# Thirteen no-operations at the head of GpSimd's program: row sums of reciprocals on one core

## The chip, the cores and the metric

The kernel runs on one core of one Trainium2 chip. A core has five engines with an instruction stream each: TensorE (PE), VectorE (DVE), ScalarE (ACT), GpSimd (POOL) and SyncE (SP). They meet at semaphores. SyncE issues the transfers between main memory and the on-chip memory of 128 partitions; sixteen DMA engines carry them. The metric is the device time of one execution in microseconds (us), as the median of several runs.

## The reference

```python
"x": np.abs(np.random.randn(32, 512, 1024)).astype(np.float32) + 1e-6

def reference(x):
    return np.sum(1.0 / x, axis=-1).astype(np.float32)
```

16,384 rows of 1,024 numbers, 64 MiB in all, are read; each row gives the sum of its reciprocals, and 64 KiB are written. The scheme leaves 128 rows of 1,024 numbers to each partition. The text calls them rows 0 to 127, and a "row" is then a tile of 128 partitions by 1,024 numbers.

## The kernel before, in words

A ring of 46 row slots (`ring`) holds the input; `sums` takes one column per row. No engine divides. ScalarE computes the reciprocal square root of a row in place (operation `A`, line 178), and somebody squares and adds it:

- `Z` (line 188): ScalarE squares and adds up itself.
- `G` and `T`: GpSimd squares the row in place (line 281), VectorE adds up (line 284).
- `Q` (line 241): VectorE squares and adds up in one instruction.
- `B` (line 256), with `K` and `M`: VectorE takes mean and variance of half rows, from which the sum of squares follows at the end.
- `P`, `U`, `L`, `E`, `R`, the pair path: 1/a + 1/b = (a + b)/(ab). GpSimd multiplies the left half of a row by its right half (`P`, line 195) into one of five product buffers (`prod`). TensorE adds the two halves by two multiplications with the identity matrix into a bank of its result memory (`U`, line 202). ScalarE turns the product into its reciprocal in two steps (`L` and `E`, line 212), and VectorE multiplies by the sum of halves and adds up (`R`, line 221). ScalarE has 512 elements twice instead of 1,024 once and a squaring.

Row 127 is split in two halves of 512 numbers.

The order is written out by hand in `PLAN`, a list of tokens; the letter is the operation, the number the row, `+n` a count of rows and `@n` the buffer or the bank. Each engine executes its own tokens in the list's order. `D` (line 170) is a load of so many rows on SyncE's queue. A load waits until the ring slots that it overwrites are free. The helper `note` drops waits that follow from others.

Where an instruction needs more semaphores than it can wait for by itself, the compiler puts wait words ahead of it, instructions of their own in the engine's program (EVENT_SEMAPHORE in the trace, "POOLq" where they are GpSimd's). A word is one instruction of a program. Counted from the head of GpSimd's program, the product of row 111 (token `P111@0`) is word 70 in the kernel before, with a wait word right ahead of it; the product of row 95 (`P95@0`) stands 13 words earlier: six products and squares and six wait words lie between the two.

The part of the list around both products:

```python
R89 B90 A92+2 P95@0 U95@5 R91 A94 B92
G93 L95 B94 A96 A97 T93 A98 B96 E95
...
L109 B106 E107 E109 R107 P111@0 U111@2 A110 B108 A112 P113@1 R109
U113@3 L111 B110 L113 E111 B112 E113
```

GpSimd's program begins with four constants and the identity matrix (`make_identity`: a memset at masks.py:197 and a select at masks.py:199, which needs a setting of the engine ahead of it). Its first square, `G1+3`, waits for ScalarE.

Of the kernel before, what the change touches and what calls it, by code (L numbers as in the profile page):

```python
# [11 lines left out]
def kernel(  # L12
# [5 lines left out]
    nc = tc.nc  # L18
    f32 = mybir.dt.float32
    P = 128  # L20
    NOPS = 0
    D = 1024
    H = D // 2
    F = 128
# [4 lines left out]
    NR = 127  # L29
    STATS = ((43, 3, 11), (80, 2, 18),)  # L30
    STORES = (0, 21, 43, 64, 81, 99, 116)
    LATE = ("A", 127)
    S = float(2**17)
    FIT = 1.0 - 2.0**-17

# [57 lines left out]
    def parse(tok):  # L93
        body, _, b = tok[1:].partition("@")
        r, _, n = body.partition("+")  # L95
        return tok[0], int(r), int(n or 1), int(b or 0)
# [4 lines left out]
    def area(u, n=1):  # L101
        r, at, w = place(u)
        if u >= NR:
            w, n = sum(place(i)[2] for i in range(u, u + n)), 1
        return ring[:, r % R : r % R + n, at : at + w]
# [5 lines left out]
    def note(engine, inst, reads=(), writes=()):  # L111
        inst = inst.ins
        known = dict(begun.get(engine, {}))  # L113
        before = {}
        for spaces, writing in ((reads, False), (writes, True)):
            for space in spaces:
                for other in history.get(space, ()):
                    if writing or other[3]:
                        before[other[0].name] = other
        needed = sorted(before.values(), key=lambda o: -o[4])  # L120
        for other in needed:
            o_inst, o_engine, o_tick, _, _, o_known = other
            if o_engine == engine:
                continue
            if o_tick <= known.get(o_engine, 0):
                tc.declare_no_dep(inst, o_inst, reason="implied by other waits")
                continue
            for e, t in o_known.items():
                known[e] = max(known.get(e, 0), t)
            known[o_engine] = max(known.get(o_engine, 0), o_tick)  # L130
        count[engine] = count.get(engine, 0) + 1
        begun[engine] = known
        entry = (engine, count[engine])
        if engine == "SP":
            entry = (f"load {count[engine]}", 1)
        for spaces, writing in ((reads, False), (writes, True)):
            for space in spaces:
                history.setdefault(space, []).append(
                    (inst, *entry, writing, sum(count.values()), known)
                )  # L140

    def rows(u, n=1):
        spaces = []
        for r, at, w in (place(i) for i in range(u, u + n)):
            spaces += [("row", r % R, i) for i in range(at, at + w, 128)]
        return spaces
# [1 line left out]
    def half(u, at):  # L148
        return [("row", u % R, i) for i in range(at, at + H, 128)]

    work = {}
    loaded = 0
    summed = set()
    slot, bank = {}, {}
# [1 line left out]
    def store(lo, hi):  # L156
        a, at = divmod(lo, HALF)
        nc.sync.dma_start(out=out_v[a, :, at : at + hi - lo], in_=sums[:, lo:hi])

    with tc.manual_schedule():  # L160
        for op, u, n, b in (parse(tok) for tok in PLAN):
            if op == "D":
                n, u = u, loaded
                while n:
# [3 lines left out]
                    if u >= NR:  # L168
                        w, k = sum(place(i)[2] for i in range(u, u + m)), 1
                    inst = nc.sync.dma_start(  # L170
                        out=area(u, m),
                        in_=x_v[r // HALF, :, r % HALF : r % HALF + k, at : at + w],
                    )
                    note("SP", inst, writes=rows(u, m))
                    u, n = u + m, n - m
                loaded = u
            elif op in "AC":
                inst = nc.scalar.activation(  # L178
                    out=area(u, n),
                    in_=area(u, n),  # L180
                    func=Arsqrt if op == "A" else Square,
                    scale=FIT if op == "A" else 1.0,
                )
                note("ACT", inst, writes=rows(u, n))
                work[op, u] = inst.ins
            elif op == "Z":
                r = place(u)[0]
                inst = nc.scalar.activation(  # L188
                    out=area(u), in_=area(u), func=Square, accum_out=sums[:, r : r + 1]
                )  # L190
                summed.add(r)
                note("ACT", inst, writes=rows(u))
            elif op == "P":
                slot[u], r = b, u % R
                inst = nc.gpsimd.tensor_tensor(  # L195
                    out=prod[:, b], in0=ring[:, r, :H], in1=ring[:, r, H:], op=mult
                )
                note("POOL", inst, rows(u), [("slot", b)])
            elif op == "U":
                bank[u], r = b, u % R  # L200
                for h in range(2):
                    inst = nc.tensor.matmul(  # L202
                        ps[:, b],
                        lhsT=ident,
                        rhs=ring[:, r, h * H : (h + 1) * H],
                        start=h == 0,
                        stop=h == 1,
                    )
                    note("PE", inst, half(u, h * H), [("bank", b)])
            elif op in "LE":  # L210
                pair = prod[:, slot[u]]
                inst = nc.scalar.activation(  # L212
                    out=pair,
                    in_=pair,
                    func=Arsqrt if op == "L" else Square,
                    scale=S * FIT if op == "L" else 1.0,
                )
                note("ACT", inst, writes=[("slot", slot[u])])
            elif op == "R":
                pair = prod[:, slot[u]]  # L220
                inst = nc.vector.tensor_tensor_reduce(  # L221
                    out=pair,
                    in0=pair,
                    in1=ps[:, bank[u]],
                    scale=S,
                    scalar=0.0,
                    op0=mult,
                    op1=add,
                    accum_out=sums[:, u : u + 1],
                )  # L230
                note("DVE", inst, [("bank", bank[u])], [("slot", slot[u])])
            elif op == "Q":
                r, at, w = place(u)
                joined = [u]
                while len(joined) < n:
# [5 lines left out]
                inst = nc.vector.tensor_tensor_reduce(  # L241
                    out=row,
                    in0=row,
                    in1=row,
                    scale=1.0,
                    scalar=total if r in summed else 0.0,
                    op0=mult,
                    op1=add,
                    accum_out=total,
# [3 lines left out]
            elif op == "B":  # L253
                i = stat_rows.index(u)
                for h in range(2):
                    inst = nc.vector.bn_stats(  # L256
                        out=stats[:, i, h], in_=ring[:, u % R, h * H : (h + 1) * H]
                    )
                    note("DVE", inst, reads=half(u, h * H), writes=[("stat", i)])
            elif op in "KM":  # L260
                lo, step, n = STATS[u]
                i = stat_rows.index(lo)
                part = stats[:, i : i + n]
                if op == "K":
                    mean = part[:, :, :, :, 1].rearrange("p f h e -> p (f h e)")
                    inst = nc.scalar.activation(  # L266
                        out=mean, in_=mean, func=Square, scale=float(H // 2) ** 0.5
                    )
                    engine = "ACT"
                else:  # L270
                    inst = nc.vector.tensor_reduce(  # L271
                        out=sums[:, lo : lo + step * (n - 1) + 1 : step],
                        in_=part[:, :, :, :, 1:].rearrange("p f h e k -> p f (h e) k"),
                        axis=mybir.AxisListType.XY,
                        op=add,
                    )
                    engine = "DVE"
                note(engine, inst, writes=[("stat", j) for j in range(i, i + n)])
            elif op == "G":
                row = area(u, n)  # L280
                inst = nc.gpsimd.tensor_tensor(out=row, in0=row, in1=row, op=mult)  # L281
                note("POOL", inst, writes=rows(u, n))
            elif op == "T":
                inst = nc.vector.tensor_reduce(  # L284
                    out=sums[:, u : u + n],
                    in_=area(u, n),
                    axis=mybir.AxisListType.X,
                    op=add,
                )
# [2 lines left out]
                for lo, hi in zip(STORES, STORES[1:]):  # L292
                    store(lo, hi)
        store(STORES[-1], F)
        for i in range(NOPS):
            inst = nc.gpsimd.nop(hint="idle", nofuse=True)
            if i == 0:
                tc.add_manual_dep(
                    inst.ins,
                    work[LATE].name,  # L300
                    mybir.DependencyInfo(
                        mybir.DependencyClass.Sync, mybir.DependencyReason.DATA
                    ),
                    reason="GpSimd idles behind the loads",
                )


# [28 lines left out]
```

## Time and profile before

| | |
|---|---|
| median of 3 runs | 166.45 us (166.45 to 166.57) |
| time of the profiled execution | 166.35 us |
| its span, first to last instruction | 164.5 us |
| ACT busy | 145.8 us, 89% |
| DVE busy | 116.0 us, 71% |
| POOL busy | 109.2 us, 66% |
| DMA, all sixteen engines | 408 GB/s over the span |

The profile is one execution. Times in it are microseconds from the start of the span. In a timeline a row is "start, duration, engine, line, operation, output<-input, count, and in brackets the engine's idle time before it and what ended it". Rows of one kind that follow each other without a gap are merged (`x2`). A `q` behind an engine's name is its sequencer, which reads the program and holds the waits. The chain of work that ended last is followed back from the last instruction; "issue" in it is time in which an engine waited for nothing that the profile shows.

A share of the DMA queues in a window is the time of the packets that start in it, over sixteen times the window. It is over 100% for a window shorter than its packets. "q1" carries loads and stores, "q14" instructions.

### The profile page before, as it was taken

How to read it: one execution, taken by the hardware profiler on the slowest of the kernel's cores; microseconds unless marked ns; L12 is line 12 of the kernel's file. 1: busy time of each engine (PE TensorE's matmuls, PEld its weight loads, DVE VectorE, ACT ScalarE, POOL GpSimd, SP SyncE). 2: the span in 40 equal slices, each digit the busy share in tenths (PEclk: the TensorE clock that was granted, in tenths of full speed). 3: DMA queues.
4: the chain of work that ended last, by engine and by line, in shares of the span. 5: the costliest groups of instructions: out<-in, count | busy, mean ns of one | idle time of the engine just before them, and what ended most of it. 6: DMA issues, size and time to landing. Idle time of an engine off the chain costs nothing.

```text
span 164.5 us, 627 instructions
## 1 busy us (share of the span) xinstructions
PE 38.9 (24%) x68; PEld 14.6 (9%) x68; DVE 116.0 (71%) x147; ACT 145.8 (89%) x148; POOL 109.2 (66%) x56
## 2 busy tenths in 40 slices
PE   0000000000000000062000000075808199699600
PEld 0000000000000000020000000031302133234100
DVE  0000003469927049999999999999698969999894
ACT  3600199999999999999999999999999999989994
POOL 1000069998999999999408979999916196377400
PEclk9999999999999999999999999999985559999985
DMA  5999899899989899899999999999999999999960
GB/s 197 488 514 394 382 430 526 382 430 430 462 351 526 351 478 450 356 478 406 438 446 390 486 398 404 454 412 464 418 422 418 427 428 423 424 410 418 408 212 2
DMA packets 4611, 67.20 MB, mean 408 GB/s; under 512 B 1408, under 2 KB 1408, under 8 KB 2176
## 3 DMA queue, kind: packets, MB, share of 16 engines
q1 hardware_dynamic: 4608, 67.18, 96.0%
q14 instruction: 3, 0.02, 0.0%
HBM read 67.11 MB, written 0.07 MB: 408 GB/s over the span
## 4 chain that ended last, share of the span: by engine, by line
ACT 63%; DMA 26%; DVE 6%; issue 2%; POOL 2%; SPq 0%; DVEq 0%; POOLq 0%
ACT ring L178 47%; DMA ring<-in_x_dram 26%; ACT ring L188 10%; ACT prod L212 6%; DVE ring L241 2%; DVE stats L256 2%; POOL prod L195 2%; DVE prod L221 1%; DVE sums L284 1%; SPq L170 0%; ACT stats L266 0%; DVE sums L241 0%; DVE sums L221 0%; DVEq L241 0%; DVEq L331 0%
## 5 line engine op out<-in xcount | busy, mean ns | idle before, releaser
L178 ACT ACTIVATE ring<-ring 128x1024 f32<-128x1024 f32 (+4 forms) x65 | 104.2, 1660 | 15.1 <-DMA ring<-in_x_dram 14.9
L281 POOL TENSOR_TENSOR ring<-ring 128x1024 f32<-128x1024 f32 (+2 forms) x33 | 85.8, 2629 | 30.4 <-ACT ring L178 30.4
L284 DVE TENSOR_REDUCE sums<-ring 128x1 f32<-128x1024 f32 (+4 forms) x27 | 53.3, 1998 | 42.2 <-POOL ring L281 42.1
L202 PE MATMUL ps<-ring,ident 128*128 128x512 f32 x68 | 38.9, 722 | 116.5 <-DMA ring<-in_x_dram 115.2
L256 DVE BATCH_NORM_STATS2 stats<-ring 128x6 f32<-128x512 f32 x58 | 36.5, 678 | 3.1 <-ACT ring L178 3.1
L195 POOL TENSOR_TENSOR prod<-ring 128x512 f32<-128x512 f32 x17 | 22.8, 1361 | 14.9 <-DMA ring<-in_x_dram 10.4
L202 PEld LDWEIGHTS ps<-ring,ident 128*128 128x128 f32 x68 | 14.6, 228 | 139.9 <-POOL ring L281 71.4
L188 ACT ACTIVATE ring<-ring 128x1024 f32<-128x1024 f32 x23 | 24.0, 1044 | 0.0
L212 ACT ACTIVATE prod<-prod 128x512 f32<-128x512 f32 x34 | 19.8, 616 | 0.5 <-POOL prod L195 0.4
L241 DVE CUSTOM_DVE_ANT_0 ring<-ring 128x1024 f32<-128x1024 f32 (+1 forms) x12 | 17.6, 1481 | 0.5 <-ACT ring L178 0.4
L221 DVE CUSTOM_DVE_ANT_0 prod<-prod,ps 128x512 f32<-128x512 f32 x17 | 11.1, 675 | 0.3 <-ACT prod L212 0.3
L188 ACT ACTIVATION_READ_ACCUMULATOR ring<-ring 128x1 f32 x23 | 4.4, 189 | 0.0
L71 ACT ACT_TABLE_LOAD x1 | 1.3, 1283 | 0.7 <-PEq L320 0.7
L221 DVE DVE_READ_ACCUMULATOR2_ANT sums<- 128x1 f32 x17 | 1.4, 80 | 0.0
L241 DVE DVE_READ_ACCUMULATOR2_ANT sums<- 128x1 f32 x13 | 1.0, 79 | 0.0
L241 DVE CUSTOM_DVE_ANT_0 ring<-ring,sums 128x512 f32<-128x512 f32 x1 | 0.8, 751 | 0.1
L266 ACT ACTIVATE stats<-stats 128x44 f32<-128x44 f32 (+1 forms) x2 | 0.5, 268 | 0.0
L271 DVE TENSOR_REDUCE sums<-stats 128x11 f32<-128x88 f32 (+1 forms) x2 | 0.5, 268 | 0.0
masks.py:197 POOL MEMSET ident<- 128x128 f32 x1 | 0.2, 205 | 0.3 <-POOLq L320 0.3
masks.py:199 POOL TENSOR_SCALAR_AFFINE_SELECT ident<-ident 128x128 f32<-128x128 f32 x1 | 0.3, 292 | 0.1
L320 POOL MEMSET const-float32-0.0<- 128x1 f32 x1 | 0.1, 98 | 0.2 <-issue 0.2
L320 POOL MEMSET const-bfloat16-1.0<- 128x1 bf16 x1 | 0.1, 101 | 0.0
(2 smaller groups left out, 0.2 us busy)
## 6 DMA issues: line engine op xcount, KB each, us to landing
ring<-in_x_dram SPq DMA_DIRECT2D x2, 6144.0 KB, 25.8
ring<-in_x_dram SPq DMA_DIRECT2D x3, 4096.0 KB, 25.9
ring<-in_x_dram SPq DMA_DIRECT2D x3, 3072.0 KB, 26.2
ring<-in_x_dram SPq DMA_DIRECT2D x1, 5632.0 KB, 56.0
ring<-in_x_dram SPq DMA_DIRECT2D x1, 5120.0 KB, 32.2
ring<-in_x_dram SPq DMA_DIRECT2D x1, 4608.0 KB, 43.3
ring<-in_x_dram SPq DMA_DIRECT2D x4, 1024.0 KB, 37.8
ring<-in_x_dram SPq DMA_DIRECT2D x1, 3584.0 KB, 24.4
```

Source lines behind the costliest of these rows:

```text
L71: nc.scalar.add_instruction(mybir.InstLoadActFuncSet(name=nc.get_next_instruction_name(), act_func_set_id=act_sets.index("abs_reciprocal_s ...
L178: inst = nc.scalar.activation(out=area(u, n), in_=area(u, n), func=Arsqrt if op == "A" else Square, scale=FIT if op == "A" else 1.0,)
L188: inst = nc.scalar.activation(out=area(u), in_=area(u), func=Square, accum_out=sums[:, r : r + 1])
L195: inst = nc.gpsimd.tensor_tensor(out=prod[:, b], in0=ring[:, r, :H], in1=ring[:, r, H:], op=mult)
L202: inst = nc.tensor.matmul(ps[:, b], lhsT=ident, rhs=ring[:, r, h * H : (h + 1) * H], start=h == 0, stop=h == 1,)
L212: inst = nc.scalar.activation(out=pair, in_=pair, func=Arsqrt if op == "L" else Square, scale=S * FIT if op == "L" else 1.0,)
L221: inst = nc.vector.tensor_tensor_reduce(out=pair, in0=pair, in1=ps[:, bank[u]], scale=S, scalar=0.0, op0=mult, op1=add, accum_out=sums[:, ...
L241: inst = nc.vector.tensor_tensor_reduce(out=row, in0=row, in1=row, scale=1.0, scalar=total if r in summed else 0.0, op0=mult, op1=add, acc ...
L256: inst = nc.vector.bn_stats(out=stats[:, i, h], in_=ring[:, u % R, h * H : (h + 1) * H])
L266: inst = nc.scalar.activation(out=mean, in_=mean, func=Square, scale=float(H // 2) ** 0.5)
L281: inst = nc.gpsimd.tensor_tensor(out=row, in0=row, in1=row, op=mult)
L284: inst = nc.vector.tensor_reduce(out=sums[:, u : u + n], in_=area(u, n), axis=mybir.AxisListType.X, op=add,)
```

## The change

Thirteen no-operations are put ahead of the list's work on GpSimd. In the built program they lie between the memset and the select of the identity matrix. By them every later word of GpSimd's program moves 13 places, so that word 70 is the product of row 95. The constants `NOPS` and `LATE`, with the loop at the end that they control, go; with `NOPS = 0` that loop had added no instruction. The other engines' programs are the same in both kernels. Lines of the file shift by one, two or twelve places.

```diff
-    NOPS = 0
+    EARLY = 13
...
-    LATE = ("A", 127)
...
-    work = {}
...
     with tc.manual_schedule():
+        for _ in range(EARLY):
+            nc.gpsimd.nop(hint="idle", nofuse=True)
         for op, u, n, b in (parse(tok) for tok in PLAN):
...
-                work[op, u] = inst.ins
...
         store(STORES[-1], F)
-        for i in range(NOPS):
-            inst = nc.gpsimd.nop(hint="idle", nofuse=True)
-            if i == 0:
-                tc.add_manual_dep(
...
```

More of the change, by code (lines that the diff above doesn't have):

```diff
@@ L294 @@
         store(STORES[-1], F)
-        for i in range(NOPS):
-            inst = nc.gpsimd.nop(hint="idle", nofuse=True)
-            if i == 0:
-                tc.add_manual_dep(
[L299 to L305, printed above, removed]
 _INS = ['x']
```

## The prediction

> **What bounds the kernel now.** I read the page's head and shares first, then the chain of work that ended last in order of time, then the timelines of GpSimd, TensorE and ScalarE around the moved word.
>
> ```profile
> span 164.5 us, 627 instructions
> PE 38.9 (24%) x68; PEld 14.6 (9%) x68; DVE 116.0 (71%) x147; ACT 145.8 (89%) x148; POOL 109.2 (66%) x56
> PE   0000000000000000062000000075808199699600
> q1 hardware_dynamic: 4608, 67.18, 96.0%
> q14 instruction: 3, 0.02, 0.0%
> ```
>
> ScalarE is busy 89% of the span and the load queue keeps the sixteen DMA engines busy 96% of it, so the kernel sits on two bounds that take turns. GpSimd, at 66%, is neither. TensorE does nothing in the first seventeen of forty slices, some 70 us. Besides the loads there are three instruction packets, 0.02 MB together. Where the turns fall is in the chain:
>
> ```profile
> 99.47 24.38 DMA ring<-in_x_dram
> 123.84 0.02 issue
> 123.87 2.86 ACT ring L178 x2
> ...
> 140.99 1.21 DVE stats L256 x2
> 142.20 0.00 POOLq L195
> 142.20 0.42 issue
> 142.62 2.52 POOL prod L195 x2
> 145.15 0.02 issue
> 145.17 1.67 ACT prod L212 x3
> ```
>
> Until 123.84 a load decides: ScalarE takes up its data at 123.87. From there to the end the chain is compute. At 142.20 GpSimd's wait word, which stands just ahead of the product of row 111, is released; the product starts only at 142.62, and those 0.42 us are "issue", time in which it waited for nothing that the profile shows. ScalarE then waits for the two products:
>
> ```profile
> 144.13 0.61 ACT L212 ACTIVATE prod<-prod 128x512 f32<-128x512 f32 x1
> 145.17 1.67 ACT L212 ACTIVATE prod<-prod 128x512 f32<-128x512 f32 x3 [0.42 <-POOL prod L195]
> 148.88 1.04 ACT L178 ACTIVATE ring<-ring 128x1024 f32<-128x1024 f32 x1
> ```
>
> It is done at 144.74 (144.13 + 0.61) and idles 0.42 us. That is its only idle time on GpSimd, and it lies on the path to the end.
>
> **The price of word 70.** How long a product normally takes to start is read by setting GpSimd beside TensorE, which waits for the same rows:
>
> ```profile
> 137.29 3.70 PE L202 MATMUL ps<-ring,ident 128*128 128x512 f32 x8 [0.28 <-DMA ring<-in_x_dram]
> 142.27 10.79 PE L202 MATMUL ps<-ring,ident 128*128 128x512 f32 x24 [1.28 <-DVE stats L256]
> 137.38 2.52 POOL L195 TENSOR_TENSOR prod<-ring 128x512 f32<-128x512 f32 x2 [1.74 <-DVE sums L284]
> 142.62 2.51 POOL L195 TENSOR_TENSOR prod<-ring 128x512 f32<-128x512 f32 x2 [2.73 <-DVE stats L256]
> ```
>
> At row 107 GpSimd starts 0.09 us behind TensorE (137.38 - 137.29), with wait words ahead of it as at row 111. At row 111 it is 0.35 behind (142.62 - 142.27). The excess is 0.26 by this comparison and 0.33 by the chain (0.42 of issue less an ordinary 0.09). I take 0.33, since the chain measures from GpSimd's own release and TensorE's start at 142.27 has its own delay in it. So word 70 costs its sequencer about 0.33 us, and row 111 shows it because a wait word stands right in front: the sequencer can't have passed word 70 earlier.
>
> **The change, part by part.** Thirteen no-operations are added. No wait is added, no DMA is issued, nothing is reordered on the other engines. Their place is ahead of the second step of the identity matrix, and what follows on GpSimd is:
>
> ```profile
> 22.08 10.57 POOL L281 TENSOR_TENSOR ring<-ring 128x3072 f32<-128x3072 f32 x2 [20.78 <-ACT ring L178]
> L195 POOLq EVENT_SEMAPHORE  x10: 17/17/43, 108.0 to 153.3; - x10
> ```
>
> The trace has no no-operation. The nearest row is GpSimd's wait words, 17 ns each, so 13 are some 0.2 us; the upper bound is what would show, 20.78 / 13 = 1.6 us each. I take 0 on the path, hidden by the 20.78 us in which GpSimd waits for ScalarE; the identity matrix, finished behind them, is wanted by TensorE only after 70 us.
>
> Word 70 becomes the product of row 95:
>
> ```profile
> 118.21 1.89 POOL L281 TENSOR_TENSOR ring<-ring 128x1024 f32<-128x1024 f32 x1 [0.26 <-ACT ring L178]
> 123.91 1.28 POOL L195 TENSOR_TENSOR prod<-ring 128x512 f32<-128x512 f32 x1 [3.81 <-DMA ring<-in_x_dram]
> 126.63 0.61 ACT L212 ACTIVATE prod<-prod 128x512 f32<-128x512 f32 x1
> ```
>
> Ahead of it GpSimd idles 3.81 us for the row's load, and no wait word lies between it and the square at 118.21. If the sequencer reads it while that square runs, 0.33 us vanish in the idle time. If the cost falls after the load has landed, the product ends at 125.52 instead of 125.19 (123.91 + 1.28), and ScalarE wants it at 126.63: 1.11 us are left. Either way it is 0 on the path; without this cover it would be 0.33.
>
> Row 111 then starts 0.33 earlier. ScalarE would take up row 113's product at 145.17 - 0.33 = 144.84, still behind its own 144.74, so the whole 0.33 reaches it, and 0.10 of the gap stays. What is late next: loads. The activation at 148.88 moves to 148.55 and needs a load that was issued at 109.81 and landed 38.5 later, at 148.31:
>
> ```profile
> 109.81 0.33 SPq L170 DMA_DIRECT2D ring<-in_x_dram  x1
> ring<-in_x_dram SPq DMA_DIRECT2D x1, 1024.0 KB, 38.5
> 151.69 0.69 DVE L221 CUSTOM_DVE_ANT_0 prod<-prod,ps 128x512 f32<-128x512 f32 x1 [0.30 <-ACT prod L212]
> 152.64 1.22 DVE L241 CUSTOM_DVE_ANT_0 ring<-ring 128x1024 f32<-128x1024 f32 x1 [0.25 <-ACT ring L178]
> ```
>
> 0.24 us stay in hand. VectorE, which writes the last sums, waits 0.30 and 0.25 us for ScalarE on the way, so it follows. I pass 0.33 on to the end.
>
> **The instruction packet moves too.** Of the three, one follows row 111 by 3.3 us, at 145.95. In narrow windows, a share times sixteen times the window is a packet's time (145.95:145.955, two rows; 146.265:146.267; then for the packet before 100.17:100.18, 100.485:100.495 and 102.06:102.064):
>
> ```profile
> q14 instruction: 1, 0.01, 397.5%
> q1 hardware_dynamic: 1, 0.01, 386.2%
> q1 hardware_dynamic: 2, 0.02, 3040.6%
> q14 instruction: 1, 0.01, 203.1%
> q1 hardware_dynamic: 1, 0.02, 983.8%
> q1 hardware_dynamic: 1, 0.02, 1428.1%
> ```
>
> At 145.95 the packet takes 0.32 us beside a load packet of 0.31. In the next window two load packets start with 0.97 us between them, so the one behind it takes 0.66, and its DMA engine loses 0.32 + 0.35 = 0.67. At 100.2 it is 0.33, and the load packet behind takes 1.57 in place of the next one's 0.91: 0.99 lost. What that does to a landing:
>
> ```profile
> 100.47 7.31 ACT L178 ACTIVATE ring<-ring 128x1024 f32<-128x1024 f32 x4
> 108.06 5.43 PE L202 MATMUL ps<-ring,ident 128*128 128x512 f32 x8 [32.88 <-DMA ring<-in_x_dram]
> 115.37 3.70 PE L202 MATMUL ps<-ring,ident 128*128 128x512 f32 x8 [1.88 <-DMA ring<-in_x_dram]
> ```
>
> These are starts on three landings with 3 MB between each pair: 7.59 us with the packet in it, 7.31 without, so 0.28 late. After the one at 145.95 nothing of the kind is seen: the activation at 148.88 didn't wait. Moved, the packet follows a word that is read between 108.0 (the first of the ten wait words) and 123.91, so by the same 3.3 us it comes between 111 and 127, and delays the landing at 123.84, on which ScalarE waits, by 0 to 0.28 us. I take 0, by the row of the same engine's packet, and keep 0.28 for the range.
>
> Sum: 0 + 0 - 0.33 + 0 = -0.33. The profiled execution took 166.35 (164.5 of span and 1.85 around it) and would take 166.02; the median of 166.45 becomes 166.12, which I give as 166.1.
>
> The skill has a rule against this: the Trainium skill, "Runtime: NRT & Kernel Launch", section "Instruction fetch mechanics", says that the sequencer fetches the next block by itself and that crossing a block boundary is one bump of the queue's tail, mostly hidden. By that rule alone word 70 would cost nothing and the time would stay at 166.45; the 0.42 us of issue, on the path, speak against "hidden" at row 111, and for it wherever the engine idles anyway.
>
> **Rivals.** *No change, 166.45.* Either the 0.42 belongs to row 111 and not to the word's number (its wait word covers a landing and VectorE), or the moved packet hands the 0.28 on: 166.45 - 0.33 + 0.28 = 166.40. Against the first: at 137.38 GpSimd also had a load and VectorE to wait for, and started 0.09 behind TensorE. For the second: ScalarE starts at 123.87, right on the landing.
>
> *Slower.* A DMA engine loses 0.67 (at 145.95) to 0.99 us (at 100.2). Where that engine is the last of the sixteen, the landing at 123.84 is late by all of it and everything behind is too: 166.45 - 0.33 + 0.67 to 0.99 = 166.79 to 167.11. It decides from 0.66 us up. For it: the landing is the path there, which it isn't at 145.95. Against it: neither of these two packets delayed a landing by more than 0.28.
>
> *More, 166.0 or less.* ScalarE's whole 0.42 goes: 166.03, and below that if VectorE's and GpSimd's rows speed up where they no longer coincide.
>
> **How the numbers follow.** 0.2% is 0.33 us, about what a measurement of this kernel can tell from no change, and the forecast lies on that mark. The forecast has 0.64 (166.0 to 166.25), of which 0.45 beyond the mark and 0.19 within, because more things can add to it than the sum has in it; more 0.05; no change 0.12; slower 0.19. That is faster 0.50, same 0.31, slower 0.19. The range goes from 165.95, the whole gap with 0.08 more, to 166.8, where the slower rival begins.
>
> **What would show it.** Right: no 0.42 of issue at row 111, GpSimd about 0.09 behind TensorE there, ScalarE's wait on GpSimd at 0.1 or gone, the instruction packet before 130, the landing at 123.84 unmoved. Wrong: the wait at row 111 as before, or ScalarE's start at 123.87 later by 0.3 or more, with everything behind it shifted.

## The result, and the profile after

| | before | changed |
|---|---|---|
| median of 11 runs each | 166.41 us | 165.98 us |
| ratio, 95% interval | | 0.9974 (0.9965 to 0.9984) |
| profiled execution | 166.35 us | 166.02 us |
| its span | 164.5 us | 164.2 us |

The changed kernel is faster by 0.26%, with an interval from 0.16% to 0.35%. A second measurement, below, gave 0.9980 (0.9971 to 0.9989). The two agree within their intervals; between the profiled executions the difference is 0.33 us, 0.2%.

The chain of work that ended last, changed kernel, in the stretch that the prediction showed (start, duration, what):

```profile
99.43 24.43 DMA ring<-in_x_dram
123.86 0.02 issue
123.88 2.86 ACT ring L178 x2
...
141.00 1.21 DVE stats L255 x2
142.21 0.09 issue
142.31 2.52 POOL prod L194 x2
144.83 0.02 issue
144.85 1.67 ACT prod L211 x3
```

The load in front lands at 123.86, before at 123.84. VectorE releases GpSimd at 142.21, before at 142.20. Up to here nothing has moved by more than 0.02 us. Then 0.09 us of issue stand where there were 0.42, and ScalarE starts at 144.85 in place of 145.17. The timelines of TensorE and GpSimd in the changed kernel, at rows 95, 107 and 111:

```profile
123.90 3.78 PE L201 MATMUL ps<-ring,ident 128*128 128x512 f32 x4 [4.82 <-DMA ring<-in_x_dram]
137.30 3.70 PE L201 MATMUL ps<-ring,ident 128*128 128x512 f32 x8 [0.71 <-DMA ring<-in_x_dram]
142.28 10.80 PE L201 MATMUL ps<-ring,ident 128*128 128x512 f32 x24 [1.28 <-DVE stats L255]
```

```profile
123.92 1.28 POOL L194 TENSOR_TENSOR prod<-ring 128x512 f32<-128x512 f32 x1 [3.80 <-DMA ring<-in_x_dram]
137.39 2.52 POOL L194 TENSOR_TENSOR prod<-ring 128x512 f32<-128x512 f32 x2 [1.74 <-DVE sums L283]
142.31 2.51 POOL L194 TENSOR_TENSOR prod<-ring 128x512 f32<-128x512 f32 x2 [2.40 <-DVE stats L255]
```

Row 111 starts 0.03 us behind TensorE, before 0.35. Row 95, the new word 70, starts 0.02 behind it, as before: its price doesn't show there. ScalarE's wait on GpSimd is no longer in its list of waits (the third wait on a load, 0.23 us at 100.67, lies ahead of the stretch in question):

```profile
ACT ring L178 <- DMA ring<-in_x_dram: 15.1, 3, 11.4
ACT L70 <- PEq L308: 0.7, 1, 0.7
```

The instruction packet, finally, is found in the window 112.13:112.14:

```profile
q14 instruction: 1, 0.01, 193.1%
```

It takes 0.31 us (193.1% of 16 times 0.01). It has come from 145.95 to 112.13, and the landing at 123.86 shows nothing of it.

### The profile page after: what moved, and what is told of

Read it like the earlier page. It is cut to its first block, busy times and chain, and to the rows that moved or that the text cites. A ratio compares the mean times of both kernels' runs of the same rounds, so it can differ in the third digit from the quotient of the medians.

```text
span 164.2 us, 640 instructions
## 1 busy us (share of the span) xinstructions
PE 38.2 (23%) x68; PEld 14.4 (9%) x68; DVE 115.9 (71%) x147; ACT 145.7 (89%) x148; POOL 108.8 (66%) x56
## 4 chain that ended last, share of the span: by engine, by line
ACT 63%; DMA 26%; DVE 6%; issue 2%; POOL 2%; SPq 0%; DVEq 0%; POOLq 0%
ACT ring L178 47%; DMA ring<-in_x_dram 26%; ACT ring L187 10%; ACT prod L211 6%; DVE ring L240 2%; DVE stats L255 2%; POOL prod L194 2%; DVE prod L220 1%; DVE sums L283 0%; SPq L170 0%; ACT stats L265 0%; DVE sums L240 0%; DVE sums L220 0%; DVEq L240 0%; POOLq L194 0%
## 5 line engine op out<-in xcount | busy, mean ns | idle before, releaser
L201 PE MATMUL ps<-ring,ident 128*128 128x512 f32 x68 | 38.2, 712 | 117.2 <-DMA ring<-in_x_dram 115.9
L194 POOL TENSOR_TENSOR prod<-ring 128x512 f32<-128x512 f32 x17 | 22.5, 1339 | 15.0 <-DMA ring<-in_x_dram 10.8
```

The lines of the kernel that those rows point to most:

```text
L194: inst = nc.gpsimd.tensor_tensor(out=prod[:, b], in0=ring[:, r, :H], in1=ring[:, r, H:], op=mult)
L201: inst = nc.tensor.matmul(ps[:, b], lhsT=ident, rhs=ring[:, r, h * H : (h + 1) * H], start=h == 0, stop=h == 1,)
```

## The experiments

All ratios are against the kernel before, on the same chip. In the executions below the loads land up to 0.3 us earlier or later than before, so single starts are compared by a distance: from TensorE's start on row 95, which follows a landing, to GpSimd's start on row 111. It is 18.73 us before (142.62 - 123.89) and 18.41 in the changed kernel (142.31 - 123.90).

The theories: W, a word's number has a price of 0.33 us, paid on the path only where nothing covers it; O, the delay belongs to row 111; P, the gain comes from the instruction packet's place; N, from the no-operations themselves.

### One no-operation

```diff
-    EARLY = 13
+    EARLY = 1
```

> One no-operation at the head in place of thirteen: word 70 is the wait word in front of the product of row 111, which GpSimd's sequencer can read while it has nothing to do, between the products of rows 109 and 111 (138.6 to 142.2 us). Theory W (the word's number costs 0.33 us wherever it stands): row 111 starts 0.1 us behind its release as with thirteen, 0.3 us gained against the kernel before, about 166.1; if the price were charged only after the wait is over, nothing is gained, 166.4. Theory O (the 0.42 us belong to row 111, and thirteen words changed something else): 166.4. Theory P (the gain comes from the instruction packet's earlier place, 112 us instead of 146): the packet moves by some 4 us only, still among the loads of the tail, so less than the 0.3 us are gained.

Measured: 166.21 against 166.46, ratio 0.9984 (0.9975 to 0.9993). The same chain, and TensorE's start on row 95:

```profile
142.44 0.09 issue
142.53 2.53 POOL prod L194 x2
```

```profile
124.08 2.93 PE L201 MATMUL ps<-ring,ident 128*128 128x512 f32 x3 [4.82 <-DMA ring<-in_x_dram]
```

The distance is 18.45. One word is enough to take the price off the path, so thirteen are not what matters; O's row 111 is as quick as any other. This speaks against P too: the packet comes at 141.66, 4.3 us earlier than before and still among the loads of the tail, and the delay is gone all the same. And in the kernel before, the late start at 142.62 lies ahead of the packet at 145.95, so the packet's transfer can't have caused it.

### The same thirteen at the end

```diff
-        for _ in range(EARLY):
-            nc.gpsimd.nop(hint="idle", nofuse=True)
         for op, u, n, b in (parse(tok) for tok in PLAN):
...
         store(STORES[-1], F)
+        for _ in range(EARLY):
+            nc.gpsimd.nop(hint="idle", nofuse=True)
```

> The same thirteen no-operations at the end of GpSimd's program, behind the last product: the program is as long as the changed one, but word 70 is the product of row 111 again. W: 166.4 as before, with 0.42 us of issue at row 111 and the instruction packet at 146 us. N and any theory by which the program's length counts: 166.1.

Measured: 166.58, ratio 1.0003 (0.9994 to 1.0012). The chain:

```profile
142.50 0.43 issue
142.93 2.52 POOL prod L192 x2
```

The whole delay is there, the distance is 18.75 (from 124.18), and the packet comes at 146.07. Neither a longer program nor thirteen words more does anything; it is their place ahead of row 111 that counts.

### Eight and nine: word 70 moved to rows 99 and 103

```diff
-    EARLY = 13
+    EARLY = 8      # then 9
```

> Eight no-operations: word 70 is the product of row 99, which starts at 131.3 us right behind two wait words, as that of row 111 did. W: here the delay must appear, 0.3 to 0.35 us more behind TensorE's start on the same row than the 0.09 us that it is before and after; ScalarE wants the two products only at 133.35 and 134.81, 0.8 and 1.0 us after they are done, so the time stays at the changed kernel's, about 166.1, with row 111 at 0.1 us behind its release. O: no delay at row 99; row 111 still 0.42 behind, 166.4.

> With eight no-operations the 0.33 us turned out to lie at the second wait word of rows 99 and 103, one word behind the product of row 99. With nine, word 70 is the product of row 99 itself. W: it starts 0.35 to 0.45 us behind its landing, 0.4 us behind TensorE's start on the same row, and ScalarE still finds it done (0.4 us to spare), so the time is that of the changed kernel. If the word counted is another one, row 99 starts 0.09 us behind TensorE as everywhere.

With eight the ratio is 0.9981 (0.9972 to 0.9990), and row 111 is quick (distance 18.40). Row 99 however wasn't late, against the expectation: 131.50, with TensorE at 131.41. GpSimd's words on line L194 (L195 before) between 131 and 132.5 us, first of the kernel before, then with eight:

```profile
L195 POOLq EVENT_SEMAPHORE  x2: 17/17/17, 131.2 to 131.3; - x2
```

```profile
L194 POOLq EVENT_SEMAPHORE  x2: 17/17/17, 131.4 to 131.8; - x2
```

The two wait words are 0.1 us apart before and 0.4 with eight. The second one stands behind row 99's product, in front of row 103's, and the expectation had taken both for row 99's. So word 70 was this wait word, read late while the product of row 99 ran. With nine it is row 99's product:

```profile
131.27 9.80 PE L201 MATMUL ps<-ring,ident 128*128 128x512 f32 x16 [3.52 <-DMA ring<-in_x_dram]
```

```profile
131.71 2.51 POOL L194 TENSOR_TENSOR prod<-ring 128x512 f32<-128x512 f32 x2 [3.82 <-DMA ring<-in_x_dram]
```

It starts 0.44 behind TensorE in place of 0.09: 0.35 for the word. The distance to row 111 is 18.42 (142.39 - 123.97), so the chain there doesn't feel it; the time, 166.09, is that of a single run. O falls: the delay goes where the number goes, to the word.

### 128 no-operations: how often a word has a price

```diff
-    EARLY = 13
+    EARLY = 128
```

> 128 no-operations at the head, some 5 us of GpSimd's 20 us of idle time there: word 70 is a no-operation and the product of row 111 is word 198. An instruction packet is 8 KB, which at 64 bytes a word would be 128 words. W with a block of 128 words: the delay is back at row 111 (0.42 us of issue), the time is that of the kernel before, 166.4, and there is one instruction packet more, four in the span. W with a block of 256 words: no delay at row 111, 166.1, three packets. Theory N (the gain comes from the no-operations themselves, by the later start of the identity matrix or of the engine): 166.1 or less, since there are more of them.

Measured: 166.45, ratio 0.9997 (0.9988 to 1.0006). The chain at row 111, the packets of the whole execution, and the no-operations that stand in four stretches of 1 us (1.05:2.05 and so on):

```profile
142.39 0.39 issue
142.78 2.53 POOL prod L194 x2
```

```profile
q14 instruction: 4, 0.03, 0.0%
```

```profile
L160 POOLq NOP  x26: 13/13/13, 1.0 to 2.0; - x26
L160 POOLq NOP  x26: 13/13/13, 2.0 to 3.0; - x26
L160 POOLq NOP  x18: 13/13/13, 3.0 to 4.0; - x18
L160 POOLq NOP  x26: 13/13/13, 4.0 to 5.0; - x26
```

Row 111 is word 198 here, and the delay is back, 0.30 us (0.39 - 0.09), with a fourth packet, at 6.63 us. So the price comes again 128 words on, at 70 and at 198. The third stretch measures it by itself: it has 8 no-operations fewer than the 26 of the others; at 1 us / 25 intervals they are 0.04 us apart, which makes 0.32 us, with nothing waiting and nothing computed beside it. The no-operations up to 3.05 us, and those from 3.40 on:

```profile
L160 POOLq NOP  x59: 13/13/13, 0.7 to 3.0; - x59
L160 POOLq NOP  x69: 13/13/13, 3.4 to 6.1; - x69
```

Together they are all 128, so the stretch doesn't just lack records: between the fifty-ninth, at 3.04, and the sixtieth, at 3.40, there is a gap of 0.37 us, 0.33 more than the usual 0.04. Counted like row 111, the sixtieth is word 70. There is no second gap up to the last one, word 138, so the price doesn't come every 64 words either (word 134 would have it). N falls with the ratio.

### 125: the price on row 115

```diff
-    EARLY = 13
+    EARLY = 125
```

> 125 no-operations: by a block of 128 words the next dear word is word 198, and that is the product of row 115, right behind its wait word, in place of the product of row 111. Theory W (a price of 0.33 us for every 128th word, paid on the path only where nothing covers it): row 111 starts 0.1 us behind its release; row 115 starts 0.42 us behind its landing and ends at about 147.6, while ScalarE wants it at 147.37, so 0.25 us of the 0.31 gained are lost again: 166.4 less 0.05, a ratio of 0.9995 to 1. Theory O (the delay belongs to row 111 alone): no delay at row 115, 0.9981 as with thirteen.

Measured: 166.38, ratio 0.9996 (0.9987 to 1.0004). GpSimd at rows 111 and 115, and ScalarE at row 115, here; then ScalarE at row 115 in the changed kernel:

```profile
142.53 2.51 POOL L194 TENSOR_TENSOR prod<-ring 128x512 f32<-128x512 f32 x2 [2.40 <-DVE stats L255]
146.53 1.28 POOL L194 TENSOR_TENSOR prod<-ring 128x512 f32<-128x512 f32 x1 [1.48 <-DMA ring<-in_x_dram]
147.84 0.63 ACT L211 ACTIVATE prod<-prod 128x512 f32<-128x512 f32 x1
```

```profile
147.38 1.27 ACT L211 ACTIVATE prod<-prod 128x512 f32<-128x512 f32 x2
```

Row 111 is quick (18.41 from TensorE's 124.12 on row 95). Row 115 is not: from row 111 to row 115 it is 4.00 us, against 3.69 in the second measurement of the changed kernel (146.08 - 142.39). The chain of this execution shows the same, the load's landing followed by the issue:

```profile
106.95 39.12 DMA ring<-in_x_dram
146.07 0.02 issue
146.09 0.04 POOLq L194
146.13 0.39 issue
```

ScalarE is 0.46 later than in the changed kernel, of which 0.22 is that this execution's loads landed later (124.12 against 123.90), so 0.24 are the price, as expected (0.25). The times say the same: 166.38 against the changed kernel's 166.14, measured beside it. One word's 0.33 us costs 0.31, 0.24 or nothing, by what stands around it.

### The changed kernel again

> The changed kernel once more, beside the other kernels of this call. All theories: 0.3 to 0.45 us under the kernel before, as in its first measurement (ratio 0.9974); by the sum of the profile, 0.31, it is 0.9981.

Measured: 166.14 against 166.46, ratio 0.9980. So the first 0.43 us between the medians shouldn't be read as more than the 0.33 of the profiled executions.

### What instruction packets cost: no-operations on ScalarE

```diff
         for _ in range(EARLY):
             nc.gpsimd.nop(hint="idle", nofuse=True)
+        for _ in range(40):      # then 16
+            nc.scalar.nop(hint="idle", nofuse=True)
```

> The changed kernel with forty no-operations more at the head of ScalarE's program, 1.6 us of the 3.4 that ScalarE idles before the first load. It asks what the instruction packets do to the loads: if ScalarE's program has the same dear word, the packet at 100.2 us, behind which the loads land 0.26 us later, moves to about 50 us, where load packets are larger and the packet at 65.7 costs its own DMA engine 0.69 us instead of 0.99. Theory: the load that lands at 123.86 lands up to 0.27 us earlier, ScalarE's row of work behind it starts up to 0.2 us earlier (it is busy almost without a gap ahead of it), 165.8 to 165.95. Rival: the packet at 100.2 isn't ScalarE's, or the engine that is last in its place is as late: landings as in the changed kernel, 166.0.

> The changed kernel with sixteen no-operations at the head of ScalarE's program, where forty brought a fourth instruction packet at 162.89 us, beside the last store, and a time of 0.35 us over the kernel before. Theory E (that packet held up the last store, which landed 2.1 us behind its issue in place of 1.4): with sixteen, ScalarE's program is too short to reach the word that calls it; three packets, the last store lands 1.4 us behind its issue, and the time is that of the changed kernel, 166.0 to 166.15, a ratio of 0.9975 to 0.998. Rival: the no-operations on ScalarE cost the time by themselves; then some of the 0.6 us between the two kernels is seen here too, 166.3 or more.

With forty: 166.78, ratio 1.0021 (1.0012 to 1.0030), slower than before, where up to 0.2 us less than the changed kernel was expected. The packet that ScalarE's words move isn't the one at 100.2 but the one at 65.8; it comes at 25.0 with forty and at 50.1 with sixteen. The load in question landed 0.09 earlier (123.77 instead of 123.86), not 0.27. And the end is where the time went, in the window 161.8:163.2, forty first, then sixteen:

```profile
q1 hardware_dynamic: 135, 0.01, 6.2%
q14 instruction: 1, 0.01, 1.7%
out_dram<-sums SPq DMA_DIRECT2D x1, 6.0 KB, 2.1
```

```profile
q1 hardware_dynamic: 144, 0.01, 6.6%
out_dram<-sums SPq DMA_DIRECT2D x1, 6.0 KB, 1.4
```

With forty an instruction packet stands beside the last store, which lands 2.1 us after its issue in place of 1.4. With sixteen there is none, the store takes 1.4 and the ratio is 0.9979 (0.9970 to 0.9988), that of the changed kernel. So sixteen no-operations on ScalarE cost nothing by themselves, and the packet at the very end cost 0.6 to 0.7 us. The trace shows where: nine of the store's 144 packets, the share of one DMA engine in sixteen, start only from 163.27 on, when the instruction packet ends (162.89 + 0.38), while the others are done at 162.94. The trace also marks when each of the store's sixteen parts has landed: fifteen by 163.30, the last at 164.03. The nine packets are 0.4 us late; why their part lands 0.7 us late stays open. No version here beats the changed kernel by more than the measurement can tell.

## Why the prediction was right, step by step

- *What bounds the kernel.* Right. The chain changed at one place, and everything behind it came 0.30 to 0.32 us earlier.
- *The price of word 70, 0.33.* Right: 0.33 by the issue that went (0.42 to 0.09), 0.32 by the missing no-operations, 0.35 at row 99. The lower figure of 0.26, by TensorE's start, was too low: TensorE's start at 142.27 was itself late by more than usual, as was suspected, since row 111 is now 0.03 behind it.
- *Thirteen no-operations, 0 on the path.* Right. They take 13 times 0.04 us, more than twice the 0.2 us taken from the wait words' length, and the select moved from 1.00 to 1.45 us; the wait for ScalarE behind it is still 20.31 us long.
- *Row 95, 0 on the path.* Right, and of its two cases it was the first: row 95 starts 0.02 behind TensorE, and the packet at 112.13 shows that the word was read long before the load landed.
- *Row 111's 0.33 passed on whole.* Right: ScalarE came 0.32 earlier (145.17 to 144.85), and no load or VectorE step took it back; the sum of 166.02 for a profiled execution was met. That it was met to the hundredth is luck: the chain's end came 0.30 earlier (162.23 to 161.93), and the rest lies outside the span.
- *The instruction packet, 0 of 0 to 0.28.* Right; the landing moved by 0.02, and with it *slower* fell. The 0.28 itself stood on one execution. By the same rows the packet at 100.2 made 0.11 in the changed kernel (108.08 - 100.67 = 7.41, against 7.30 from there to 115.38) and 0.01 in its second measurement (7.31 against 7.30), so 0.28 was the largest of three readings and not what such a packet always costs. That a packet can cost on the path was shown only where the last store waited on it (forty on ScalarE).
- *No change* as a rival had two forms, and both fell: the 0.42 doesn't belong to row 111, since the delay went to whichever word was number 70 (row 99's product with nine no-operations), and the moved packet handed nothing back.
- The Trainium skill ("Runtime: NRT & Kernel Launch", section "Instruction fetch mechanics") calls the crossing of a block boundary mostly hidden and gives a block of 256 instructions. Fully hidden, it would have left the time at 166.45. Here the price was hidden in the changed kernel, at row 95, and not in the one before, at row 111; and it came back 128 words on, not 256.
- *Faster beyond the mark of 0.2% rather than within* was argued weakly ("more things can add to it"). The profile gives no such thing; of the two ratios, 0.9974 lies beyond the mark and 0.9980 on it, where the sum of 0.33 lay. That the first came out beyond is luck.

What stays open: what the sequencer does in the 0.33 us (an instruction packet followed each time, which suggests that it is the fetching of the program, but no run separates the two), why a packet follows its word by 3 to 4 us (142.2 to 145.95 before), and which engine the packet at 100.2 us serves. It wasn't moved by words on GpSimd or ScalarE; words on VectorE weren't tried.

## What to carry to other kernels

Look in the chain for "issue" just ahead of an instruction that a wait word precedes, and compare it with the same instruction elsewhere: a third of a microsecond too much there can be the price of the word's number. One harmless word ahead of it, where the engine idles, moves the price onto a word that nobody waits for; any number that puts it on a covered word does as well as another. Count how far the program then reaches, because 128 words on the price and its packet come again, and at the very end of the execution the packet can hold up the last store.

## What the hardware showed that was not expected

- On GpSimd the price returns at a distance of 128 words: 0.32 to 0.35 us at word 70, 0.30 to 0.31 at word 198, with an instruction packet of 8 KB each time. One word more or less takes it to the neighbour.
- A no-operation takes 13 ns by its row on GpSimd but 0.04 us of the sequencer's time.
- ScalarE's program has a packet of its own: sixteen words on ScalarE moved the packet at 65.8 us to 50.1, forty to 25.0 and called up one more at 162.89, which cost the last store 0.7 us.
